# Page visits of up to three units in two banks, joined index sums and key scores, a later hand-over of weight loads and a tail on three engines, in a one-core decoder step

## The chip, the core and the metric

One Trainium2 chip, one of its cores. The metric is the device time of one execution in microseconds (us): the median of several runs, and beside it one execution under the hardware profiler. The engines are TensorE (PE; PEld is its weight load), VectorE (DVE), ScalarE (ACT), GpSimd (POOL) and SyncE (SP), which issues most DMAs.

## The reference

One layer of a decoder step for 256 prompt tokens and 64 sample tokens (8 requests of 8 tokens; NT = 320 columns in all), all in float32. One input projection feeds three groups of heads, and one output projection and a LayerNorm end the layer:

```python
aq, ak, av, ag, iq, ik, iw, bq, bf, bi, bg, mq, mg = _in_proj(h, w_in, pos)      # 2048 -> 8272 columns, rotary on q, k
sc   = _indexer_scores(iq, iw, ik_all)       # sum over 16 heads of w * relu(q . k): the index head sums
_, sel = lax.top_k(sc, n_sel)                # 256 of 2056 keys for a sample token, 64 of 256 for a prompt token
a_out = _sparse_attend(q, k[sel], v[sel], valid)     # 8 heads x 128; a sample token's keys lie in 16 pages of 128
b_o, s = _hgrn2(bq, bf, bi, lb, s0, chunk)   # gated linear recurrence, 4 heads
m_out = _mem_attend(mq, mk, mv)              # cross-attention into 256 memory tokens, 4 heads
cat   = concatenate([a_out * silu(ag), rms(b_o) * silu(bg), m_out * silu(mg)])
y     = layernorm(ALPHA * h + cat @ w_out)
```

The cached keys, values and index keys of the 8 requests are read through a page table; the selection is a mask over all past keys, so every page is read once.

## The kernel before

**Wide work.** The projections run as matmuls of 128x128 weights on 320 (or 256, 512) columns. Each float32 weight is split in two parts (wh and wl, rounded float32r), so each product is three matmuls: wh with xh, wh with xl, wl with xh. A weight entry of 512 KB lands in a buffer `wr` (three of them), ACT casts a half to `wh`, DVE or POOL subtracts to `wl` (four buffers each), and PE uses the halves in quanta of two row blocks. The list `wspec` fixes the order of the entries: input projection with the memory projection in it, then the output projection (`wo`), whose rows come from `cat` after `split` has cut them into the same two parts.

**Narrow work.** The sample tokens of one request pair give 32 columns, so their attention runs as matmuls with 128x32 weights: four groups (two requests, two halves of heads) beside each other. For each of four pairs p there are eight units of keys (K, two pages of each request) and eight of values (V); two units each of cross keys (XK) and cross values (XV) serve the memory. A key unit writes 256 columns of a bank `kv`; two make 512 scores, which ACT copies to S. A value unit adds to the bank `va`. The kernel calls a stretch of units on PE a visit.

**What sets the order.** The kernel writes its program with a planner (`Plan`) that keeps a time for each engine and tile. The main loop at the end asks `units_now` whether a visit of pages is due: before, two units if both are there, one if the next weight half is not ready or it has waited `PATIENCE`. Else PE gets the next quantum of `wspec`. All other work stands in generators in the list `bg`, which `background` resumes when their wants (`need(...)`) are met; a want with `visit=` is held for so many us until a visit comes, and then `join_visit` resumes it right behind the visit. `new_keys` (scores of a pair's 8 new keys against its queries) is such a one; the recurrence and parts of the extraction are others. The index head sums (`sums` in `idx_sample`) are written by the next step of the index scores. `loads` decides what SP issues: a weight goes as soon as `plan.slot_free("wr", 3) <= plan.now + 1`, that is up to 1 us before the planner believes its buffer free; pages go when a buffer `pg` or `S` is free and the planned DMA queue is less than 4 us ahead; at most LOOK units ahead. SP issues in order, so an issue that waits for its buffer holds up what is behind it.

**The tail.** `finish_sample` normalises the last 64 rows, laid out as 128 x 1024 in `r`: DVE subtracts the mean and multiplies by g, and then multiplies by the inverse deviation and adds b, each in a piece of 640 and one of 384 columns, and SP stores each piece.

In the kernel's lines below a helper issues every instruction, so that all stand at one line in the profile (L157 before, L160 after); instructions are told apart by tile names.

Of the kernel before, what the change touches and what calls it, by code (L numbers as in the profile page):

```python
# [36 lines left out]
RES = 7  # L37
PACE = 4.8
HOMES = 5
EARLY = [(2, 1), (2, 3), (2, 5), (2, 6), (2, 7)]  # L40
PATIENCE = 9.0
SOON = 0.4
LAG = 1.5
LAG2 = 0.8
VISIT_WAIT = 9.0
HASTE = 2.0
CALM = 4.0
IDLE = 3.0
LOOK = 3
TABLES = {AF.Exp: "exp_ln", AF.Ln: "exp_ln", AF.Silu: "silu", AF.Sqrt: "sqrt"}  # L50
EXP_LN = 6
PORT = ("tensor_tensor", "tensor_add", "tensor_sub", "tensor_mul", "scalar_tensor_tensor", "tensor_scalar", "tensor_copy",
# [93 lines left out]
class Engine:  # L146
# [41 lines left out]
    def cost(self, op, outs, ins, n):  # L188
        if self.name == "PE":
            n, a = math.prod(outs[0].shape[1:]), ins[0]  # L190
            shape = tuple(next(w for w in (32, 64, 128) if m <= w) for m in (a.shape[0], math.prod(a.shape[1:])))
            turn = 0.0
            if shape != self.shape:
                turn = 0.31 if shape == (128, 128) else 0.09 if self.shape == (128, 128) else 0.2
                self.shape = shape
            if op == "transpose":
                return turn + 0.109
            if a.dtype == F32R:
                return turn + 0.0087 + n * 0.0004325
# [29 lines left out]
def hymba_step(ctx: ExitStack, tc: tile.TileContext, I, O):  # L229
# [483 lines left out]
    def key_scores(p, u, ps):  # L713
# [5 lines left out]
        return  # L719
        yield  # L720

    def unit(n):
        kind, p, u = punits[n]
        tl = [PG.pop((n, b)) for b in range(2)]
# [2 lines left out]
        if kind == "K":  # L727
# [1 line left out]
                S[p] = new([128, PAST + NS], "S")  # L729
                plan.pinned.add(S[p].tensor.name)  # L730
            if u % 2 == 0:
                st["kv"] = PS([128, 512], "kv")
            c = 256 * (u % 2)
            for hh in range(2):
                for h2 in range(2):
# [8 lines left out]
        elif kind == "V":  # L744
            if u == 0:
                VACC[p] = PS([128, 512], "va")
            for j in range(2):
                kt = 2 * u + j
                for b, hp, g in GROUPS:
                    PE.matmul(VACC[p][g:g + 32, :], PTt[p][:, kt, g:g + 32], pair(tl[b][:, j, :], hp),  # L750
                              start=kt == 0, stop=False)
            if u == 7:
                for b, hp, g in GROUPS:
                    PE.matmul(VACC[p][g:g + 32, :], PTt[p][:, 16, g:g + 32], pair(avS, hp),
                              start=False, stop=True)
                bg.insert(0, [extract(p), need(VACC[p], ps=0)])
                done.add(("vdone", p))
        elif kind == "XK":
            if p == 0:
                st["xk"] = PS([128, 512], "kv")  # L760
            ps = st["xk"][:, 256 * p:256 * p + 256]
            for h in range(4):
                for b in range(4):
                    PE.matmul(ps[32 * b:32 * b + 32, :], st["mqpad"][:, 4 * p + b, h, :],
                              tl[b // 2][:, b % 2, 256 * h:256 * h + 256], start=h == 0, stop=h == 3)
            if p == 1:
                for g in range(2):
                    bg.insert(0, [xsoft(g, st["xk"][:, 256 * g:256 * g + 256]), need(st["xk"], ps=0)])
        else:
            va = PS([128, 512], ("va", "kv")[p])  # L770
            for nt in range(2):
                for b in range(4):
                    PE.matmul(va[32 * b:32 * b + 32, :], st["xpt", p][:, nt, 32 * b:32 * b + 32],
                              tl[b // 2][:, b % 2, 512 * nt:512 * nt + 512], start=nt == 0, stop=nt == 1)
            bg.insert(0, [xextract(p, va), need(va, ps=0)])
            if p == 1:
                free(st["mqpad"])

    def unit_ready(n):
# [1 line left out]
        if any((n, b) not in PG or plan.avail(PG[n, b]) > plan.now for b in range(2)):  # L781
            return False
        if kind == "K":
            return u % 2 or ("aq", 7) in done and plan.slot_free("kv", 1) <= plan.now and (
                u or plan.slot_free("S", BUFS["S"]) <= plan.now and len(S) + len(in_s) + ci_live(1) < BUFS["S"]
                and (p < BUFS["S"] or ("soft", p - BUFS["S"]) in done))
        if kind == "V":
# [12 lines left out]
    def units_now(n):  # L800

        if not unit_ready(n):
            return 0
        kind, p, u = punits[n]
        if u % 2 or kind[0] == "X" and p:
            return 1
        if loaded(n + 1) and (kind != "V" or u < 6 or "attn" in done):
            return 2
        if kind[0] == "X":
            return 0  # L810
        if since[0] is None:
            since[0] = plan.now
        return int(not half_soon() or plan.now > since[0] + PATIENCE)

    def half_soon():
        if half >= len(wspec) or half not in WH:
# [100 lines left out]
    def idx_sample():  # L917
# [26 lines left out]
        more = new([128, 2048], "pg")  # L944
        plan.split.add(more.tensor.name)
        st["more"] = 1
        slots = [t[:, 512 * i:512 * i + 512] for t in (early, more) for i in range(4)]
        used = [0]

# [4 lines left out]
        def sums(sp, rs):  # L954

            for c in sorted({c for c, f in rs}):
                ps = PS([128, 512], "va")
                for f in (1, 0):
                    for g in range(4):
                        PE.matmul(ps[32 * g:32 * g + 32, :], wpad[sp][:, g, f, :], rs[c, f][g], start=f == 1, stop=f == 0)  # L960
                d = sc[:, 512 * c:512 * c + 512]
                if sp:
                    DVE.tensor_add(d, d, ps)
                else:
                    ACT.copy(d, ps)

        def new_tokens():

# [48 lines left out]
        while not keys_in(0):  # L1017
            yield
        kk = stack(0)
        rs, full = {}, None  # L1020
        for k, (sp, c, f, a) in enumerate(steps):
            n = kk[0].shape[-1]
            yield need(ql, qh, *kk, ps=2, lag=LAG2)
# [3 lines left out]
                PE.matmul(pd[j][:, 0:n], qh[:, b], kk[j], start=True, stop=False)  # L1027
                PE.matmul(pd[j][:, 0:n], qlr[:, b], kk[j], start=False, stop=True)
            if full:
                sums(*full)  # L1030
                if (sp, c) == (0, 1):
                    new_sums()
                full = None
            r = rs.setdefault((c, f), [])
            for j in range(2):
                r.append(relu_slot(n))
# [2 lines left out]
                else:  # L1039
                    DVE.tensor_scalar(r[-1], pd[j][:, 0:n], 0.0, None, op0=OP.max)  # L1040
            if a == 1 and f == 0:
                full, rs = (sp, rs), {}
            while not keys_in(k + 1):
                yield
            if k + 1 < len(steps):
                kk = stack(k + 1)
                yield
        yield need(*[x for r in full[1].values() for x in r], ps=1)
        sums(*full)
        del st["more"]  # L1050
        free(ql, qh, *st.pop("wpad"))
        done.add("idxdone")
# [148 lines left out]
    def new_keys(p):  # L1201

        yield from wait(("ak", 7))
        while p not in S:
            yield
        yield need(akS, st["qpad"], visit=VISIT_WAIT)
        ps = PS([128, NS])
        for hh in range(2):
            for h2 in range(2):
# [52 lines left out]
    def extract(p):  # L1262
# [2 lines left out]
        o = [T(256), T(256)]  # L1265
        for i in range(2):
            ACT.activation(o[i], VACC[p][:, 256 * i:256 * i + 256], AF.Copy, scale=RS[p][:, 1:2])
        del VACC[p], PTt[p]
        yield from wait(("gate", 7))
        yield need(*o)  # L1270
# [625 lines left out]
    def finish_sample():  # L1896
# [3 lines left out]
        DVE.bn_aggr(out=s[0:64, 0:2], in_=bn[0:64])  # L1900
        ACT.activation(s[0:64, 2:3], s[0:64, 1:2], AF.Sqrt, bias=eps[0:64, 1:2])
        DVE.tensor_copy(s[64:128, 0:1], s[0:64, 0:1])
        for cs in (slice(0, 640), slice(640, 1024)):
            DVE.scalar_tensor_tensor(r[:, cs], r[:, cs], s[:, 0:1], gb[:, 0, cs], op0=OP.subtract, op1=OP.mult)
            if cs.start == 0:
                DVE.reciprocal(s[0:64, 2:3], s[0:64, 2:3])
                ACT.copy(s[64:128, 2:3], s[0:64, 2:3])
        for cs in (slice(0, 640), slice(640, 1024)):
            DVE.scalar_tensor_tensor(r[:, cs], r[:, cs], s[:, 2:3], gb[:, 1, cs], op0=OP.mult, op1=OP.add)
            SP.dma_start(O["ys"][:, cs], r[:, cs])  # L1910


# [122 lines left out]

    asked = {}

    def met(want):
        deps, nps, lag, _ = want
        return all(plan.avail(a) + lag <= plan.now for a in deps) and (not nps or n_free("mA") + n_free("mB") >= nps)  # L2040

    def resume(e):
        asked.pop(e[0], None)
# [7 lines left out]
    def join_visit():  # L2051

        for e in list(bg):
            if e[1] and e[1][3] and met(e[1]):
                resume(e)

    def loads():
        nonlocal nw, npg
        while True:
            if plan.t["SP"] > plan.now + 0.5:  # L2060
                return
            if nw < len(wspec) and wspec[nw].get("ref"):
                nw += 1
                continue
            if nw < len(wspec) and nw < half + 5 and plan.slot_free("wr", 3) <= plan.now + 1 and nw - nprep < 3 \
                    and (wspec[nw]["kind"] != "mem" or has_room(3)):
                load_w(nw)
                nw += 1
# [203 lines left out]
```

## Time and profile before

| | us |
|---|---|
| median of 3 runs | 855.14 (854.65 to 855.36) |
| the profiled execution | 854.57 |
| its span, first to last instruction | 852.8 |
| granted TensorE clock | 0.997 |

Busy time and DMA by stage, from the trace (share of the 16 DMA engines, GB/s):

| stretch, us | PE | DVE | ACT | POOL | DMA | GB/s |
|---|---|---|---|---|---|---|
| 0 to 100 | 98.29 | 78.83 | 52.03 | 54.31 | 0.69 | 225 |
| 100 to 360 | 260.00 | 203.28 | 135.61 | 127.70 | 0.88 | 327 |
| 360 to 480 | 120.00 | 62.23 | 56.96 | 28.56 | 0.99 | 382 |
| 480 to 530 | 50.00 | 29.43 | 25.44 | 14.94 | 1.00 | 382 |
| 530 to 700 | 170.00 | 91.38 | 84.30 | 43.11 | 1.00 | 383 |
| 700 to 730 | 30.00 | 16.47 | 14.84 | 7.87 | 0.78 | 280 |
| 730 to 845 | 114.83 | 67.78 | 52.67 | 47.47 | 0.53 | 165 |

How to read the lines that follow: a row of the timeline is start and duration in us, engine, line, operation, out<-in by tile name, `rows*columns` of the weight, size of what is written, and a count where equal ones are merged. A float32 matmul is recorded twice. Durations of matmuls overlap: what counts on PE is the step from one start to the next.

### The profile page before, as it was taken

How to read it: one execution, taken by the hardware profiler on the slowest of the kernel's cores; microseconds unless marked ns; L12 is line 12 of the kernel's file. 1: busy time of each engine (PE TensorE's matmuls, PEld its weight loads, DVE VectorE, ACT ScalarE, POOL GpSimd, SP SyncE). 2: the span in 40 equal slices, each digit the busy share in tenths (PEclk: the TensorE clock that was granted, in tenths of full speed). 3: DMA queues.
4: the chain of work that ended last, by engine and by line, in shares of the span. 5: the costliest groups of instructions: out<-in, count | busy, mean ns of one | idle time of the engine just before them, and what ended most of it. 6: DMA issues, size and time to landing. Idle time of an engine off the chain costs nothing.

```text
span 852.8 us, 19150 instructions
## 1 busy us (share of the span) xinstructions
PE 843.1 (99%) x6892; PEld 718.0 (84%) x6892; DVE 553.9 (65%) x1100; ACT 422.3 (50%) x908; POOL 326.0 (38%) x333
## 2 busy tenths in 40 slices
PE   9999999999999999999999999999999999999996
PEld 8999999877889898878778788787887889888885
DVE  7788897744897898654474556557545343953655
ACT  6454565553555543634544554554444353744432
POOL 0677562564634445331142214333311110714424
PEclk9999999999999999999999999999999999999998
DMA  9567456889999999999989999999999988756633
GB/s 342 172 189 228 156 172 251 279 307 411 376 389 397 335 327 359 398 360 403 389 330 409 408 353 389 401 397 377 347 409 400 364 324 291 272 171 199 195 99 123
DMA packets 83216, 266.49 MB, mean 312 GB/s; under 512 B 10481, under 2 KB 21170, under 8 KB 82482
## 3 DMA queue, kind: packets, MB, share of 16 engines
q1 hardware_dynamic: 82098, 263.18, 83.6%
q0 software_dynamic: 1024, 2.10, 0.8%
q8 instruction: 54, 0.88, 0.4%
q14 instruction: 40, 0.33, 0.1%
HBM read 256.50 MB, written 8.73 MB: 311 GB/s over the span
## 4 chain that ended last, share of the span: by engine, by line
PE 98%; DMA 1%; DVE 0%; SPq 0%; ACT 0%; DVEq 0%; issue 0%
PE pj L157 57%; PE mB L157 13%; PE va L157 10%; PE mA L157 10%; PE kv L157 8%; DMA S<-in_first 1%; DVE pg L157 0%; SPq L157 0%; ACT xh L157 0%; ACT PT L157 0%; DVE s L157 0%; DVEq L2258 0%; DVE avn L157 0%
## 5 line engine op out<-in xcount | busy, mean ns | idle before, releaser
L157 ACT CAST wh<-wr 128x512 fp32r<-128x512 f32 x334 | 205.0, 621 | 243.5 <-PE pj L157 183.9
L157 PE MATMUL pj<-xh,wh 128*128 128x320 f32 (+1 forms) x992 | 313.6, 316 | 0.0
L157 PE MATMUL pj<-xh,wl 128*128 128x320 f32 (+1 forms) x992 | 303.9, 306 | 0.0
L157 PE MATMUL pj<-xl,wh 128*128 128x320 f32 (+1 forms) x992 | 303.8, 306 | 0.0
L157 DVE TENSOR_TENSOR wl<-wr,wh 128x512 fp32r<-128x512 f32 x222 | 172.7, 785 | 181.9 <-ACT wh L157 166.5
L157 POOL TENSOR_TENSOR wl<-wr,wh 128x512 fp32r<-128x512 f32 x112 | 151.0, 1357 | 240.2 <-ACT wh L157 222.7
L157 PEld LDWEIGHTS pj<-xh,wh 128*128 128x128 f32 x992 | 186.7, 188 | 16.0 <-issue 12.5
L157 PEld LDWEIGHTS pj<-xl,wh 128*128 128x128 f32 x992 | 186.8, 188 | 1.3
L157 PEld LDWEIGHTS pj<-xh,wl 128*128 128x128 f32 x992 | 186.6, 188 | 0.0
L157 POOL TENSOR_TENSOR t<-t,t 128x256 f32<-128x256 f32 (+3 forms) x53 | 46.2, 873 | 119.5 <-ACT t L157 60.0
L157 PE MATMUL va<-pg,PT 128*32 128x512 f32 x456 | 58.4, 595 | 0.0
L157 PE MATMUL kv<-pg,qpad 128*32 128x256 f32 (+1 forms) x916 | 57.5, 380 | 0.0
L157 PEld LDWEIGHTS kv<-pg,qpad 128*32 128x32 f32 (+1 forms) x916 | 30.8, 110 | 20.4 <-issue 1.3
L157 PEld LDWEIGHTS va<-pg,PT 128*32 128x32 f32 x456 | 14.6, 109 | 30.4 <-issue 28.1
L157 DVE MAX8 PT<-PT 128x8 f32<-128x1032 f32 x32 | 39.5, 1234 | 0.5
L157 DVE MATCH_REPLACE8 PT<-PT 128x1032 f32<-128x1032 f32 x32 | 39.0, 1218 | 0.0
L157 POOL DMA_INDIRECT S<-in_ci,row x24 | 25.5, 1064 | 20.0 <-DVE row L157 10.6
L157 PE MATMUL mB<-t,wh 128*128 128x256 f32 x128 | 24.5, 289 | 0.0
L157 POOL TENSOR_TENSOR bp<-t,bp 128x128 f32<-128x128 f32 (+1 forms) x17 | 10.7, 627 | 36.0 <-ACT bp L157 36.0
L157 DVE TENSOR_TENSOR cat<-S,cat 64x512 fp32r<-64x512 f32 x24 | 19.5, 813 | 6.9 <-ACT cat L157 6.4
L157 POOL TENSOR_TENSOR t<-t,tabm 128x320 f32<-128x320 f32 x16 | 14.5, 908 | 24.4 <-DVE t L157 24.2
L157 POOL TENSOR_TENSOR xl<-cat,xh 128x256 fp32r<-128x256 f32 x12 | 12.5, 1061 | 24.8 <-ACT xh L157 24.8
(430 smaller groups left out, 1355.0 us busy)
## 6 DMA issues: line engine op xcount, KB each, us to landing
wr<-in_wt SPq DMA_DIRECT2D x124, 512.0 KB
pg<-in_ck SPq DMA_DIRECT2D x114, 512.0 KB
pg<-in_cv SPq DMA_DIRECT2D x114, 512.0 KB
wr<-in_wo SPq DMA_DIRECT2D x36, 512.0 KB
wr<-in_wm SPq DMA_DIRECT2D x16, 512.0 KB
S<-in_ck SPq DMA_DIRECT2D x14, 512.0 KB
S<-in_cv SPq DMA_DIRECT2D x14, 512.0 KB
pg<-in_cXV SPq DMA_DIRECT2D x8, 512.0 KB
```

Source lines behind the costliest of these rows:

```text
L157: res = f(*a, **k)
```

## The change

- **Visits.** `units_now` lets a visit take up to VISIT = 3 units, and waits for a further one that will land within NEAR = 3 us, unless PATIENCE is over or no weight half is ready. `follows` says which unit may join. LOOK goes from 3 to 4.
- **Two banks.** Once the index scores are done, key units use the banks `kv` and `va` in turn; the accumulator of the values is pinned in `va` meanwhile.
- **Joining.** `sums_at_visit` puts the index head sums into `bg` with a visit's want, and whichever comes first, a visit or the next step, writes them; `new_keys` waits up to 18 us, not 9, for a visit; `join_visit` measures against the end of the visit.
- **Hand-over.** A weight's load is given to SP 0.6 us after the planner believes its buffer free, where it was 1 us before.
- **Planned cost** of a float32r matmul: n/2400 + 0.0133 us, where it was 0.0004325 n + 0.0087.
- **Tail.** DVE centres the last 320 columns first; ACT scales them and POOL adds b, while DVE centres and scales the other 704.

```diff
-LOOK = 3
+TAIL = 320
+VISIT = 3
+NEAR = 3.0
+LOOK = 4
@@ Engine.cost
-                return turn + 0.0087 + n * 0.0004325
+                return turn + 0.0133 + n / 2400
@@
+    def key_bank(u):
+        return ("kv", "va")[u // 2 % 2] if "idxdone" in done else "kv"
@@ unit
-                st["kv"] = PS([128, 512], "kv")
+                st["kv"] = PS([128, 512], key_bank(u))
...
                 VACC[p] = PS([128, 512], "va")
+                plan.pinned.add(VACC[p].tensor.name)
@@ units_now
-        if u % 2 or kind[0] == "X" and p:
-            return 1
-        if loaded(n + 1) and (kind != "V" or u < 6 or "attn" in done):
-            return 2
         if kind[0] == "X":
-            return 0
+            return 1 if p else 2 if loaded(n + 1) else 0
+        k, most = 1, min(VISIT, len(punits) - n)
+        while k < most and loaded(n + k) and follows(n, n + k):
+            k += 1
         if since[0] is None:
             since[0] = plan.now
-        return int(not half_soon() or plan.now > since[0] + PATIENCE)
+        if plan.now > since[0] + PATIENCE or not half_soon():
+            return k
+        if k < most and follows(n, n + k) and all((n + k, b) in PG and plan.avail(PG[n + k, b]) < plan.now + NEAR for b in range(2)):
+            return 0
+        return k if k > 1 else 0
+
+    def follows(n, m):
+        kind, p, u = punits[m]
+        if kind == "V":
+            return u and (u < 7 or "attn" in done)
+        if kind == "K":
+            return u % 2 or u and plan.slot_free(key_bank(u), 1) <= plan.now and (
+                key_bank(u) != key_bank(u - 2) or punits[n][2] == u)
+        return False
@@ idx_sample
+        def sums_at_visit(k, rs):
+            yield need(*[x for r in rs.values() for x in r], visit=VISIT_WAIT)
+            if full and full[0][2] == k:
+                sums(*full.pop()[0:2])
...
             if a == 1 and f == 0:
-                full, rs = (sp, rs), {}
+                full.append((sp, rs, k))
+                if k + 1 < len(steps):
+                    bg.insert(0, [sums_at_visit(k, rs), None])
+                rs = {}
@@ new_keys
-        yield need(akS, st["qpad"], visit=VISIT_WAIT)
+        yield need(akS, st["qpad"], visit=2 * VISIT_WAIT)
@@ finish_sample
-        for cs in (slice(0, 640), slice(640, 1024)):
-            DVE.scalar_tensor_tensor(r[:, cs], r[:, cs], s[:, 0:1], gb[:, 0, cs], op0=OP.subtract, op1=OP.mult)
...
+        centre(rest_c)
+        DVE.reciprocal(s[0:64, 2:3], s[0:64, 2:3])
+        ACT.copy(s[64:128, 2:3], s[0:64, 2:3])
+        ACT.activation(r[:, rest_c], r[:, rest_c], AF.Copy, scale=s[:, 2:3])
+        POOL.tensor_add(r[:, rest_c], r[:, rest_c], gb[:, 1, rest_c])
+        centre(most)
+        DVE.scalar_tensor_tensor(r[:, most], r[:, most], s[:, 2:3], gb[:, 1, most], op0=OP.mult, op1=OP.add)
+        for cs in (most, rest_c):
             SP.dma_start(O["ys"][:, cs], r[:, cs])
@@ join_visit
-            if e[1] and e[1][3] and met(e[1]):
+            if e[1] and e[1][3] and met(e[1], max(plan.now, plan.t["PE"] - 0.4)):
@@ loads
-            if nw < len(wspec) and nw < half + 5 and plan.slot_free("wr", 3) <= plan.now + 1 and nw - nprep < 3 \
+            if nw < len(wspec) and nw < half + 5 and plan.slot_free("wr", 3) <= plan.now + (-0.6) and nw - nprep < 3 \
```

What this does to the order of the instructions, at three places.

PE, in the key pages, the new key scores of two pairs (akS is the tile of new keys, qpad that of the padded queries, 32x64 what one writes; pj is the input projection). Before, between two products of the projection:

```order
L157 MATMUL pj_3362<-xl,wh_3356 128x320
L157 MATMUL pj_3362<-xh,wl_3357 128x320
L157 MATMUL mB_3474<-akS,qpad_411 32x64 x16
L157 MATMUL mA_3491<-akS,qpad_411 32x64 x16
L157 MATMUL pj_3362<-xh,wh_3356 128x320
```

After, right behind a visit of two key units, the first in bank kv and the second in va; the end of the second and what follows:

```order
L160 MATMUL va_3432<-pg_3174,qpad_411 32x256 x2
L160 MATMUL va_3432<-pg_3239,qpad_411 32x256 x2
L160 MATMUL mB_3449<-akS,qpad_411 32x64 x16
L160 MATMUL mA_3466<-akS,qpad_411 32x64 x16
L160 MATMUL pj_3345<-xh,wh_3317 128x320
L160 MATMUL pj_3345<-xl,wh_3317 128x320
```

The two groups moved from a stretch of their own to the end of a stretch of pages. The same holds for the other two pairs.

PE, at the change from the input projection (pj) to the output projection (mA<-wh,xh). Before, the last rows of the one and the first of the other; the transposes that extract the last cross values (ident) stand 132 products ahead of these, and the visit of the cross values 144:

```order
L157 MATMUL pj_9673<-xh,wh_9669 128x320
L157 MATMUL pj_9673<-xl,wh_9669 128x320
L157 MATMUL pj_9673<-xh,wl_9670 128x320
L157 MATMUL mA_9777<-wh_9690,xh 128x512
L157 MATMUL mA_9777<-wh_9690,xl 128x512
L157 MATMUL mA_9777<-wl_9691,xh 128x512
```

After, the transposes stand right between the two:

```order
L160 MATMUL pj_9621<-xl,wh_9611 128x320
L160 MATMUL pj_9621<-xh,wl_9612 128x320
L160 MATMUL mA_9770<-ident,t_9730 128x128 x2
L160 MATMUL mA_9770<-ident,t_9731 128x128 x2
L160 MATMUL mA_9797<-wh_9640,xh 128x512
```

and the visit itself (va from tiles S and pg, 32x512) stands between the last weight but one (wh_9572 is its last half) and the last (wh_9592 and wh_9611):

```order
L160 MATMUL pj_9621<-xh,wh_9572 128x320
L160 MATMUL pj_9621<-xl,wh_9572 128x320
L160 MATMUL pj_9621<-xh,wl_9573 128x320
L160 MATMUL va_9672<-S_9415,t_9543 32x512 x2
L160 MATMUL va_9672<-pg_9455,t_9543 32x512 x2
```

So the visit moved from 144 wide products ahead of the output projection to 24 ahead of it.

SP, in the key pages (wr is a weight's buffer, pg a page's, in_ck the cached keys, ISA the setting of a page's address). Before:

```order
L157 DMA wr_2122<-in_wt 128x1024
L157 TENSOR_LOAD ptab x3
L157 DMA wr_2169<-in_wt 128x1024
L157 DMA out_kT<-t_2125 128x320
L157 ISA
L157 DMA pg_2190<-in_ck 128x1024
```

After:

```order
L160 DMA wr_2112<-in_wt 128x1024
L160 TENSOR_LOAD ptab x3
L160 ISA
L160 DMA pg_2159<-in_ck 128x1024
L160 ISA
L160 DMA pg_2159<-in_ck 128x1024
L160 DMA wr_2174<-in_wt 128x1024
```

The page moved ahead of the second weight.

More of the change, by code (lines that the diff above doesn't have):

```diff
@@ L783, in unit_ready @@
         if kind == "K":
-            return u % 2 or ("aq", 7) in done and plan.slot_free("kv", 1) <= plan.now and (
+            return u % 2 or ("aq", 7) in done and plan.slot_free(key_bank(u), 1) <= plan.now and (
                 u or plan.slot_free("S", BUFS["S"]) <= plan.now and len(S) + len(in_s) + ci_live(1) < BUFS["S"]
@@ L946, in idx_sample @@
         st["more"] = 1
+        full = []
         slots = [t[:, 512 * i:512 * i + 512] for t in (early, more) for i in range(4)]
@@ L965, in sums @@
                     ACT.copy(d, ps)
+            if (sp, c) == (0, 1):
+                new_sums()
+        def sums_at_visit(k, rs):
+            yield need(*[x for r in rs.values() for x in r], visit=VISIT_WAIT)
+            if full and full[0][2] == k:
+                sums(*full.pop()[0:2])
         def new_tokens():
@@ L1019, in idx_sample @@
         kk = stack(0)
-        rs, full = {}, None
+        rs = {}
         for k, (sp, c, f, a) in enumerate(steps):
@@ L1029, in idx_sample @@
             if full:
[L1030 to L1033, printed above, removed]
+                sums(*full.pop()[0:2])
             r = rs.setdefault((c, f), [])
@@ L1041, in idx_sample @@
             if a == 1 and f == 0:
-                full, rs = (sp, rs), {}
+                full.append((sp, rs, k))
+                if k + 1 < len(steps):
+                    bg.insert(0, [sums_at_visit(k, rs), None])
+                rs = {}
             while not keys_in(k + 1):
@@ L1047, in idx_sample @@
                 yield
-        yield need(*[x for r in full[1].values() for x in r], ps=1)
-        sums(*full)
+        yield need(*[x for r in full[0][1].values() for x in r], ps=1)
+        sums(*full.pop()[0:2])
         del st["more"]
@@ L1267, in extract @@
             ACT.activation(o[i], VACC[p][:, 256 * i:256 * i + 256], AF.Copy, scale=RS[p][:, 1:2])
+        plan.pinned.discard(VACC[p].tensor.name)
         del VACC[p], PTt[p]
@@ L1902, in finish_sample, with centre @@
         DVE.tensor_copy(s[64:128, 0:1], s[0:64, 0:1])
-        for cs in (slice(0, 640), slice(640, 1024)):
+        tail = 1024 - TAIL
+        most, rest_c = slice(0, tail), slice(tail, 1024)
+        def centre(cs):
             DVE.scalar_tensor_tensor(r[:, cs], r[:, cs], s[:, 0:1], gb[:, 0, cs], op0=OP.subtract, op1=OP.mult)
[L1905 to L1909, printed above, removed]
+        centre(rest_c)
[6 more added lines that the diff above has]
+        for cs in (most, rest_c):
             SP.dma_start(O["ys"][:, cs], r[:, cs])
@@ L2036, in hymba_step, with met @@
     asked = {}
-    def met(want):
+    def met(want, now=None):
         deps, nps, lag, _ = want
-        return all(plan.avail(a) + lag <= plan.now for a in deps) and (not nps or n_free("mA") + n_free("mB") >= nps)
+        return all(plan.avail(a) + lag <= (now or plan.now) for a in deps) and (not nps or n_free("mA") + n_free("mB") >= nps)
     def resume(e):
```

## Prediction

> **What bounds the kernel now.** I read the head of the page first, then its chain of work that ended last.
>
> ```profile
> span 852.8 us, 19150 instructions
> PE 843.1 (99%) x6892; PEld 718.0 (84%) x6892; DVE 553.9 (65%) x1100; ACT 422.3 (50%) x908; POOL 326.0 (38%) x333
> ...
> PE 98%; DMA 1%; DVE 0%; SPq 0%; ACT 0%; DVEq 0%; issue 0%
> ```
>
> TensorE is busy from start to end and the chain never leaves it for long. A busy PE is no proof by itself, since matmul ends are modelled, so I asked for PE's own waits. There are two, both within the first 11 us:
>
> ```profile
> PE kv L1947 <- DVE t L157: 1.1, 1, 1.1
> PE va L157 <- ACT PT L157: 0.6, 1, 0.6
> ```
>
> So the time is the sum of the steps from one matmul's start to the next one's, plus about 8 us of tail. No matmul is removed by the change. Its effect can come from three things only: fewer changes between wide matmuls (128*128) and narrow ones (128*32), waits of PE that go or come, and the tail.
>
> **The price of a visit.** A visit is a run of narrow matmuls between wide ones. This is the timeline of PE around one that computes index head sums, start first:
>
> ```profile
> 203.22 0.31 PE L157 MATMUL pj<-xh,wh 128*128 128x320 f32 x1
> ...
> 204.39 0.31 PE L157 MATMUL pj<-xh,wl 128*128 128x320 f32 x1
> 204.63 0.63 PE L157 MATMUL va<-cat,t 128*32 128x512 f32 x3
> ...
> 205.09 0.60 PE L157 MATMUL va<-cat,t 128*32 128x512 f32 x3
> ...
> 205.94 0.60 PE L157 MATMUL va<-pg,t 128*32 128x512 f32 x3
> ...
> 206.49 0.41 PE L157 MATMUL pj<-xh,wh 128*128 128x320 f32 x1
> 206.74 0.31 PE L157 MATMUL pj<-xl,wh 128*128 128x320 f32 x1
> ```
>
> A wide step is (204.39 - 203.22)/8 = 0.146 us. Narrow matmuls start four at a time (three from cat and one from pg in these rows), and each of them is recorded twice, so the visit of eight is four sets; from 205.09 to 205.94 are two, 0.425 each. From 204.39 to 206.74 are 2.35 us; two wide steps (0.29) and four sets (1.70 to 1.72) leave **0.34 us** that the change of shape costs, on the way in, on the way out and in the first wide step after it.
>
> **Visits, counted.** In PE's order before I count 46 visits: 17 of key pages (cross keys among them), 18 of value pages, 4 of index head sums, 3 of new key scores, 4 of the recurrence. After: 18, 17, 4, 0 and 3, so 42. Two things stand out. Only two visits take three units (both of values), and the key visits, now spread over two banks, have become one more. And the index head sums still stand in four visits of their own: where they come due, no page visit stands between them and the next step of the scores, which adds them itself. What joined are the new key scores of all pairs, and one group of the recurrence. **4 x 0.34 = -1.36 us.**
>
> Against it stands that a visit that ends in transposes is cheaper to leave. Here PE comes straight from a key visit:
>
> ```profile
> 254.54 0.55 PE L157 MATMUL mA<-ident,t 128*128 128x128 f32 x3
> 254.84 0.39 PE L157 MATMUL pj<-xh,wh 128*128 128x320 f32 x1
> 255.07 0.31 PE L157 MATMUL pj<-xl,wh 128*128 128x320 f32 x1
> ```
>
> The first wide step takes 0.23 (254.84 to 255.07) where it took 0.25 above (206.49 to 206.74). I take 0.05 in all for such an exit, since the rows don't show what of the way out the transposes hide as well (an estimate; its bounds are 0.02, and 0.17, half the price). Nine visits end so, in transposes or mask matmuls, before, and seven after: **+0.1** (0.04 to 0.34).
>
> **Waits on the path.** In the stretch where the output projection begins there is a small one that the list of PE's waits, which leaves out gaps under its limit, shows at the weight load only:
>
> ```profile
> PEld mA L157 <- POOL wl L157: 0.5, 1, 0.5
> ```
>
> and that PE's timeline has there as two long steps:
>
> ```profile
> 736.26 0.39 PE L157 MATMUL mA<-wh,xl 128*128 128x512 f32 x1
> 736.68 0.50 PE L157 MATMUL mA<-wl,xh 128*128 128x512 f32 x1
> 737.01 0.39 PE L157 MATMUL mB<-wh,xh 128*128 128x512 f32 x1
> ```
>
> 0.42 and 0.33, where such a step takes 0.23 (0.146 x 512/320): 0.3 us. Here ACT, DVE and POOL split cat for the projection and prepare weights together. After, the cross value visit stands between the last two weights of the input projection, so the split, which starts when the first of these is through, has that visit (about 4 us) more ahead of the projection. Against it, ACT loads a table more there. I take **-0.2** (0 to -0.3).
>
> **Hand-over of weights.** The load of a weight buffer is now given to SP 1.6 us later by the planner's clock. Before, it is given so early that SP stands waiting for the buffer:
>
> ```profile
> SPq L157 <- DVE wl L157: 154.2, 79, 6.3
> SPq L157 <- POOL wl L157: 129.3, 54, 6.5
> ```
>
> 133 waits of 2.1 us on average (the columns are us in total, times, the longest), with every page, store and number of a page queued behind. 1.6 us of later hand-over comes out of them for the most part, so a weight lands little later, and what stands behind it sooner. And there is stock:
>
> ```profile
> ACT wh L157 <- PE pj L157: 183.9, 166, 4.9
> ACT wh L157 <- DMA wr<-in_wt: 11.2, 8, 2.1
> ```
>
> ACT's casts wait 166 times for PE to give a buffer back, 8 times for a weight: a load that is up to 1.6 us late is covered by that stock. **0 us**. If the cover were gone, a late weight would cost PE up to 1.6 us; on the other side stand at most the 0.8 us that PE's weight loads wait for value pages (row in the second rival), which an earlier page could take away. Later bank changes, the pins on the accumulator and the longer visit wait of the new keys issue nothing on PE that is not counted.
>
> **The shared tail.** Before, DVE alone centres and scales 640 and 384 columns:
>
> ```profile
> L157 DVE SCALAR_TENSOR_TENSOR pg<-pg,s,pg 128x640 f32<-128x640 f32 x2 | 1.8, 878 | 0.0
> L157 DVE SCALAR_TENSOR_TENSOR pg<-pg,s,pg 128x384 f32<-128x384 f32 x2 | 1.2, 599 | 0.0
> ```
>
> The timeline has their order, and SP's the issue of the two stores:
>
> ```profile
> 846.84 0.89 DVE L157 SCALAR_TENSOR_TENSOR pg<-pg,s,pg 128x640 f32<-128x640 f32 x1
> 847.64 0.15 DVE L157 RECIPROCAL s<-s 64x1 f32<-64x1 f32 x1
> 847.72 1.92 DVE L157 SCALAR_TENSOR_TENSOR pg<-pg,s,pg 128x384 f32<-128x384 f32 x3
> ```
>
> ```profile
> 849.13 0.86 SPq L157 DMA_DIRECT2D out_ys<-pg  x2
> ```
>
> A column costs (878 - 599)/256 = 1.09 ns, so 320 take 0.53 us and 704 take 0.95; each starts 0.07 to 0.09 before the last ends. After: centre 320 from 846.84, reciprocal 847.29, centre 704 from 847.37, scale 704 from 848.24 to 849.19. The larger store is issued at 849.22, against 849.13. So the share given away buys nothing on the path: before, the first store waited for 640 + 384 + 640 columns, now for 320 + 704 + 704, 64 more. ACT's copy and scale of 320 columns end about 848.25 (reciprocal done 847.44, copy 0.2, scale 0.5 to 0.6), and then POOL's add comes up against DVE:
>
> ```profile
> 842.57 1.30 POOL L157 TENSOR_TENSOR S<-S,pg 128x512 f32<-128x512 f32 x1 [4.49 <-ACT S L157]
> ...
> 843.82 1.95 POOL L157 TENSOR_TENSOR S<-S,pg 128x512 f32<-128x512 f32 x1
> ```
>
> and on DVE at the time of the second:
>
> ```profile
> 843.97 0.67 DVE L157 TENSOR_TENSOR S<-S,pg 128x512 f32<-128x512 f32 x1
> ```
>
> The same POOL add took 1.30 alone and 1.95 with a DVE add of 0.67 in it: one stood for the other. If DVE's scale (848.24) is first, POOL's add (1.30 x 320/512, 0.8 to 0.9) ends near 850.1 and the smaller store goes at 850.1, against 849.66, into a queue in which the larger still moves: **+0.1** on the end, +0.45 at most if the end follows the second issue.
>
> [...]
>
> **Sum.** -1.36 + 0.1 - 0.2 + 0 + 0.1 = -1.4 us. The profiled execution took 854.57, 0.6 under the median of the three runs (855.14), with 1.8 us outside its span; it would take 853.2, and the median becomes **853.7 us**. A measurement of this kernel can tell about 0.2%, 1.7 us, from no change, so this lies just inside "no change".
>
> **Rivals.**
> 1. It gains more: the wait at 736 goes whole, exits and tail cost nothing: -1.36 - 0.3 = -1.7, 853.4, on the border of what can be told. The runs before spread over 0.7 us, so a true -1.4 can also be measured beyond it. For it: PE is the whole chain, so every saved switch counts. Against: no row has a fifth visit to save.
> 2. Slower, through late pages. In the stretch of the value visits the DMA engines are full, and three visits already begin on the landing of a tile:
>
> ```profile
> 530.00:700.00 170.00, 170.00 (x1489) 135.36 (x1482) 91.38 (x202) 84.30 (x206) 43.11 (x50) 1.00 1.00 383
> ```
>
> (the last two figures of a stretch are the DMA engines' share and GB/s), and
>
> ```profile
> PEld va L157 <- DMA pg<-in_cv: 0.8, 3, 0.3
> ```
>
> After, the last visits stand nearer to the output projection: 24 wide matmuls lie behind the cross values, 144 before. PE's order is fixed, so if the stream of pages slips by one unit (two tiles of 1.05 MB, 5.5 us at 383 GB/s), PE stands for it: -1.4 + 5.5, 859.2. It decides from 3.1 us of waits on. Against: SP is freer, and the planner orders the visits by the landing of pages.
> [...]
> 4. The change does not do what it says. For the sums this is so by PE's order, and counted above; had the four joined too, it would be another -1.36, 852.3.
>
> **How the numbers follow.** The forecast (853.0 to 854.3) has 0.43, the first rival 0.30 (half of it the spread of runs), the third 0.15, the second 0.12. The range reaches from 852.6, the first rival with the 0.8 us of page waits gone, to 856.5, the third rival with one weight late (1.6) and the dearer exits (0.3); what the second gives above that lies outside. Faster by over 0.2%: 0.30; within: 0.58; slower: 0.12.
>
> **What would show it.** Right: PE's wide steps 0.146 as now, the new key scores without a wide matmul ahead of them, 0.34 us less for each joined group; no wait of PE near the first projection matmuls; DVE's two 704-column steps end near 4.3 us after the last matmul ends, POOL's add behind them. Wrong: PE waits for pg, S or wr tiles, a wait of over 1 us anywhere after 11 us, or a tail over 0.5 us longer. If the time falls by more than 2 us, the price of a visit or the count of what PE waits for was too small.

## The result, and the profile after

| | before | after |
|---|---|---|
| median of 6 runs each, us | 854.89 (854.36 to 855.52) | 861.52 (860.50 to 862.41) |
| the profiled execution, us | 854.57 | 860.91 |
| its span, us | 852.8 | 859.2 |

The ratio is 1.0076, 95% interval 1.0066 to 1.0086: slower by 6.6 us, where 853.7 was forecast. The head of the page and its chain of work that ended last:

```profile
span 859.2 us, 19158 instructions
PE 845.2 (98%) x6892; PEld 721.2 (84%) x6892; DVE 550.8 (64%) x1095; ACT 426.3 (50%) x911; POOL 330.0 (38%) x338
...
PE 36%; DVE 1%; ACT 0%; issue 0%; ACTq 0%; DVEq 0%
```

PE does the same 6892 matmuls in 2 us more of busy time, and a span 6.4 us longer. The chain is followed back only some 320 us here (its shares add up to 37%), but it now runs through DVE and ACT, which means that PE waited for them. The list of PE's waits says so outright (us in total, times, the longest):

```profile
PE mB L160 <- ACT t L160: 1.9, 1, 1.9
PE kv L1983 <- DVE t L160: 1.1, 1, 1.1
PE va L160 <- ACT PT L160: 0.8, 1, 0.8
PE mB L160 <- DVE s L160: 0.5, 1, 0.5
PE mA L160 <- DVE s L160: 0.4, 1, 0.4
```

The second and third stand in the first 11 us, as before. The first is new. None is for a page or for a weight to land; two more rows of 0.2 us follow in the list, one of them for ACT's cast of a weight. PE's timeline at the new wait:

```profile
591.76 0.71 PE L160 MATMUL mA<-bp,t 128*128 128x512 f32 x2
594.42 0.73 PE L160 MATMUL mB<-bp,t 128*128 128x512 f32 x2 [1.95 <-ACT t L160]
594.99 0.42 PE L160 MATMUL pj<-xh,wh 128*128 128x320 f32 x1
595.21 0.47 PE L160 MATMUL pj<-xl,wh 128*128 128x320 f32 x1
595.48 0.47 PE L160 MATMUL pj<-xh,wl 128*128 128x320 f32 x1
595.74 0.47 PE L160 MATMUL pj<-xh,wh 128*128 128x320 f32 x1
...
598.41 0.33 PE L160 MATMUL pj<-xh,wh 128*128 128x320 f32 x1
598.58 0.31 PE L160 MATMUL pj<-xl,wh 128*128 128x320 f32 x1
```

Two things are to be seen. The two state updates of the recurrence (mA<-bp,t and mB<-bp,t, twice 512 columns each) stand right behind each other, and the second waits 1.95 us. And the wide steps behind it take 0.26 to 0.27 (595.21 to 595.48 to 595.74) where such a step takes 0.15. The table by stretches (length, busy time of PE, PEld, DVE, ACT and POOL, then the granted clock, the DMA share and GB/s) tells why:

```profile
592.00:594.00 2.00, 0.47 (x2) 0.03 (x1) 1.49 (x6) 0.76 (x3) 0.62 (x1) 1.00 1.03 399
594.00:596.00 2.00, 1.58 (x6) 1.49 (x7) 1.10 (x5) 0.70 (x2) 0.00 (x0) 0.76 1.02 376
596.00:598.00 2.00, 2.00 (x7) 1.61 (x7) 0.32 (x2) 0.15 (x1) 0.00 (x0) 0.50 1.01 374
598.00:600.00 2.00, 2.00 (x14) 2.00 (x13) 0.55 (x1) 1.47 (x3) 0.46 (x1) 0.89 1.02 297
```

PE's clock is granted at half for 3.4 us after the wait (0.24, 0.50 and 0.11 of three stretches of 2 us of PE's clock are lost, which is 1.7 us). What kept ACT and DVE:

```profile
592.51 1.12 DVE L160 SCALAR_TENSOR_TENSOR bp<-bp,eG,mA 128x128 f32<-128x128 f32 x4 [1.42 <-PE mA L160]
593.55 0.75 DVE L160 COPY t<-mB 128x256 f32<-128x256 f32 x2
```
```profile
593.99 0.70 ACT L160 COPY t<-mB 128x256 f32<-128x256 f32 x2 [1.25 <-DVE t L160]
```

The two banks mB still hold the memory keys. Their copies stand on DVE behind the four updates of the first half, which wait for PE's first state update. So PE asks for a bank that can't be empty before its own last work has gone through DVE.

The tail after (DVE, ACT, POOL, SP, one timeline, cut):

```profile
850.07 0.28 PE L160 MATMUL kv<-wl,qpad 128*128 128x256 f32 x1
...
852.33 0.55 DVE L160 SCALAR_TENSOR_TENSOR pg<-pg,s,pg 128x320 f32<-128x320 f32 x1
...
852.87 2.57 DVE L160 SCALAR_TENSOR_TENSOR pg<-pg,s,pg 128x704 f32<-128x704 f32 x2
...
853.84 0.86 POOL L160 TENSOR_TENSOR pg<-pg,pg 128x320 f32<-128x320 f32 x1 [1.37 <-DVE pg L160]
855.47 0.81 SPq L160 DMA_DIRECT2D out_ys<-pg  x2
```

Both 704-column steps should end 1.9 after 852.87; they end 2.57 after it. Taken apart, the first took 0.92, and the second, recorded from 853.89 on, 1.55. From the last matmul's start to the end of the span are 859.2 - 850.1 = 9.1 us, before 852.8 - 844.6 = 8.2.

### The profile page after: what moved, and what is told of

It is laid out like the page before. It is cut to its first block, busy times and chain, and to the rows that moved or that the text cites. A ratio compares the mean times of both kernels' runs of the same rounds, so it can differ in the third digit from the quotient of the medians.

```text
span 859.2 us, 19158 instructions
## 1 busy us (share of the span) xinstructions
PE 845.2 (98%) x6892; PEld 721.2 (84%) x6892; DVE 550.8 (64%) x1095; ACT 426.3 (50%) x911; POOL 330.0 (38%) x338
## 5 line engine op out<-in xcount | busy, mean ns | idle before, releaser
L160 DVE TENSOR_TENSOR wl<-wr,wh 128x512 fp32r<-128x512 f32 x222 | 170.8, 779 | 181.4 <-ACT wh L160 173.5
L160 POOL TENSOR_TENSOR t<-t,t 128x256 f32<-128x256 f32 (+3 forms) x58 | 51.3, 885 | 119.0 <-DVE t L160 61.0
L160 PE MATMUL kv<-pg,qpad 128*32 128x256 f32 x580 | 34.1, 380 | 0.0
L160 PEld LDWEIGHTS kv<-pg,qpad 128*32 128x32 f32 x580 | 19.6, 110 | 12.0 <-issue 2.4
L160 POOL TENSOR_TENSOR bp<-t,bp 128x128 f32<-128x128 f32 (+1 forms) x19 | 12.8, 673 | 30.4 <-ACT bp L160 30.3
L160 PE MATMUL va<-pg,qpad 128*32 128x256 f32 x368 | 24.2, 380 | 0.0
L160 DVE TENSOR_TENSOR cat<-S,cat 64x512 fp32r<-64x512 f32 x24 | 17.2, 715 | 10.6 <-ACT cat L160 10.1
```

Source lines behind the costliest of these rows:

```text
L160: res = f(*a, **k)
```

## The experiments

Each was timed in several rounds beside the kernel before on its chip; the ratio is to that. "Both repairs" are those of the first two runs together.

| run | what it is | median us | ratio to before, 95% interval |
|---|---|---|---|
| e1 | after, bank repair | 858.17 | 1.0037 (1.0023 to 1.0050) |
| e2 | after, old tail | 860.10 | 1.0064 (1.0050 to 1.0077) |
| e3 | after, old price of a wide matmul | 868.40 | 1.0151 (1.0137 to 1.0165) |
| e4 | before, new tail | 855.61 | 1.0007 (0.9998 to 1.0016) |
| e5 | after, both repairs | 857.54 | 1.0031 (1.0019 to 1.0044) |
| e6 | e5, one key bank | 857.49 | 1.0028 (1.0018 to 1.0038) |
| e7 | e5, early hand-over | 865.99 | 1.0116 (1.0095 to 1.0137) |
| e8 | before, bank repair and joins | 864.52 | 1.0108 (1.0092 to 1.0123) |
| e9 | before, bank repair and later hand-over | 858.09 | 1.0037 (1.0023 to 1.0050) |
| e10 | before, bank repair, joins, new price, later hand-over | 863.74 | 1.0099 (1.0084 to 1.0114) |
| e11 | e6 with the old price | 863.82 | 1.0103 (1.0088 to 1.0119) |
| e12 | e5 without three table loads | 856.66 | 1.0019 (1.0010 to 1.0028) |

**e1, the planner's book of banks.** `Plan.slot` gives a new tile the bank whose last use is oldest, and enters the old tile's time as the new one's. When the two accumulators of the memory keys are claimed at once, the first carries the older of two old times, and the second strikes the first from the list. This is the planner's own record of it (its clock):

```
mB_1076 now 529.614 takes mB_1021 last 505.539   other in use: mB_1022 505.95
mB_1077 now 529.614 takes mB_1076 last 505.539   other in use: mB_1022 505.95
mB_1245 now 591.632 takes mB_1022 last 505.947   other in use: mB_1077 593.91
```

So at 591.6 it believed mB_1022's bank free, while the chip's bank still held mB_1076. The kernel before strikes a tile off in the same way (mB_1083 at 535.2 by the planner's clock), but claims the next bank mB only at 607.4, when the other of that pair had been read, at 603.3.

```diff
-                pj["m"] = [PS([128, 512], w) for w in ("mB", "mB", "pj", "pj")]
+                pj["m"] = []
+                for w in ("mB", "mB", "pj", "pj"):
+                    pj["m"].append(PS([128, 512], w))
+                    plan.r[pj["m"][-1].tensor.name] = plan.now
```

> The changed kernel with one correction in the planner's book of PSUM banks: the two accumulators of the memory keys are entered as in use from the moment they are claimed, so that the second doesn't strike the first off the list. The order is the changed kernel's up to the second state update of the recurrence at 592 us, which then finds its bank really taken and stands later. Theory A (the planner believed a bank free that was still to be read; PE stood 1.95 us for it, and its clock then ran at half for nearly 4 us): the wait and the slow stretch go, 2.1 + 1.7 = 3.8 us less than the changed kernel, about 857.7 us, mean granted clock back at 0.997. Rival B (the bank is not the cause; DVE and ACT are late there anyway, and PE will wait for them at the next place): 0 to 1 us less, 860.5 to 861.5, and a wait of over 1 us on DVE or ACT between 585 and 605 us. Rival C (the wait goes, but the slow clock had another cause): 2.1 us less, 859.4.

Measured 858.17, 3.35 less than the changed kernel. PE now puts six wide matmuls between the two updates and takes a bank mA:

```profile
593.93 0.71 PE L160 MATMUL mA<-bp,t 128*128 128x512 f32 x2
594.48 0.31 PE L160 MATMUL pj<-xh,wh 128*128 128x320 f32 x1
...
595.36 0.62 PE L160 MATMUL mA<-bp,t 128*128 128x512 f32 x2
```

The wait and the half clock are gone (granted clock of the run 0.997). Theory A holds, 0.4 short of its size. The profiled execution, at 859.24 the longest of the five, has another wait that the changed kernel's doesn't have, 0.9 us for ACT at 488 us, ahead of the repaired place.

**e2 and e4, the tail.** The old tail in the changed kernel, and the new tail in the kernel before:

```diff
-        centre(rest_c)
-        DVE.reciprocal(...); ACT.copy(...)
-        ACT.activation(r[:, rest_c], r[:, rest_c], AF.Copy, scale=s[:, 2:3])
-        POOL.tensor_add(r[:, rest_c], r[:, rest_c], gb[:, 1, rest_c])
-        centre(most)
-        DVE.scalar_tensor_tensor(r[:, most], ...)
+        for cs in (slice(0, 640), slice(640, 1024)):   # both steps on DVE
...
```

> The changed kernel with the tail of before (DVE alone centres and scales 640 and 384 columns). All else is as in the changed kernel. [...] Rival B (the tail differs by the larger share of DVE alone, 64 columns, 0.1 us): 861.4.

> The kernel before with the new tail alone. [...] Rival B (only the 64 columns more on DVE count): 855.0, ratio 1.000.

e2: 860.10, 1.4 less; e4: 855.61 beside 854.76 in the same group, 0.85 more, though its interval reaches no change. The traces leave no doubt on the size: from the last matmul's start to the end are 8.2 us with the old tail (before and e2) and 9.1 with the new (after), 0.9 apart, where rival B had 0.1; the span of e4 is 853.9, of before 852.8. e2 keeps the wait at the state update, with a difference:

```profile
592.85 0.71 PE L160 MATMUL mA<-bp,t 128*128 128x512 f32 x2
595.51 0.73 PE L160 MATMUL mB<-bp,t 128*128 128x512 f32 x2 [1.95 <-ACT t L160]
596.08 0.31 PE L160 MATMUL pj<-xh,wh 128*128 128x320 f32 x1
596.22 0.31 PE L160 MATMUL pj<-xl,wh 128*128 128x320 f32 x1
...
597.94 0.31 PE L160 MATMUL pj<-xh,wh 128*128 128x320 f32 x1
```

The same wait, and no slow step behind it. From the second update to the same wide matmul are 597.94 - 595.51 = 2.43 us here and 598.41 - 594.42 = 3.99 above: where the half clock follows, it costs 1.6 us more. That half clock was missing in this execution of e2 can be why it gained more than the tail's 0.9.

**e3, the price of a wide matmul.** One number of the planner back to its old value:

```diff
-                return turn + 0.0133 + n / 2400
+                return turn + 0.0087 + n * 0.0004325
```

> The changed kernel with the planner's old price of a wide matmul (0.0087 us and 0.4325 ns a column in place of 0.0133 us and 1/2400 us a column: 1.5% dearer at 512 columns). Theory A (the old price was a hidden margin: the planner's clock fell 5 us behind the chip in the course of the kernel, so what it believed ready was ready; the new price takes the margin away): the waits of PE after 11 us go back from 7.5 to about 3 us, with the half clock gone, and the time falls by 4 to 5 us less 3 visits more (44 against 41, 1.0 us): 857 to 858.5. Rival B (the waits come from the new order of the visits, whatever the price): the waits stay between 5 and 9 us, time 860 to 864.

Measured 868.40: both times missed, and theory A has fallen. A new wait leads the list:

```profile
PE va L160 <- DMA S<-in_ck: 3.5, 1, 3.5
```

The old price is no margin. The waits of PE after 11 us add up to 7.7 us, as rival B said, and the clock ran at half for 10.2 us, which rival B didn't count. The old price makes the planner believe PE later than it is: in its record the last matmuls of the kernel before stand some 5 us too late, measured from the first. That PE therefore comes to the page before it has landed is argued and not shown. By 508 us, ahead of the late page, the old price had moved the planner's clock, measured against the traces, only 1.1 us from where it stood in the changed kernel, and e10 below has late pages with the new price.

**e5, both repairs.**

> The changed kernel with both repairs: the two accumulators of the memory keys entered as in use when claimed, and the tail of before. Theory A (bank and tail are separate and add up): 861.5 - 3.4 - 0.85 = 857.3 us, still 2.4 above the kernel before; left over are the other waits (about 2 us more than before, most of it between 500 and 560 and between 715 and 740 us) and visits that save 0.6 in place of 1.26. Rival B (the waits shift from place to place, the repairs don't add up): 858.2 or more. Rival C (the two were all that was wrong, the rest is spread): 853.7.

857.54, which is 4.0 us less than the changed kernel, where theory A said 4.2; taken singly the two repairs gave 3.35 and 1.4. Single executions lie between 856.06 and 858.93, and the interval reaches to 858.7, so rival B's 858.2 isn't excluded.

**e6, one key bank** (`key_bank` returns "kv" always).

> As the run with both repairs, but all key scores in one bank as before (key_bank gives kv always). PE's order has 41 visits as with two banks, and five stretches fewer that leave the wide matmuls (93 against 98; transposes stand beside visits again). Theory A (a group of transposes that stands alone costs 0.1 to 0.3 us more than beside a visit): 0.5 to 1.5 us less than with two banks, 856 to 856.8. Rival B (the second bank spares waits for the eviction of the first): slower than with two banks, 857.5 or more, with waits of PE for DVE or ACT at the key visits (150 to 360 and 500 to 545 us).

857.49, no difference, and no wait of PE for the eviction of a key bank: neither theory. The second bank neither costs nor brings anything that shows.

**e7 to e11, other parts alone.** Their edits are those of the diff, taken back or made alone (e7: `plan.now + 1`; e8: `sums_at_visit`, `2 * VISIT_WAIT` and the shift in `join_visit` alone; e9: `plan.now + (-0.6)` alone; e10: those of e8 and e9 with the new price; e11: the old price). e8 to e10 have the old rule for visits, LOOK = 3 and one key bank; all five have the old tail and the bank repair.

> As the run with both repairs, but with the early hand-over of weight loads of before (plan.now + 1). PE's order has 43 visits against 41. Theory A (the hand-over itself costs nothing, only the two visits count, 0.7 us, and the order of the rest is a matter of luck): 857 to 859. Theory B (the later hand-over makes weights late and so the waits on ACT and DVE): waits of PE after 11 us back to about 2 us as before, 856 or less.

> The kernel before (its tail, hand-over, price of a wide matmul, visits of two units, one key bank) with the bank repair and the joins alone: index head sums and new key scores wait longer for a visit, and what is to join may come due until 0.4 us before PE ends the visit. PE's order has 43 visits against 45 and one stretch more. Theory A (a joined visit is worth 0.34 us, as the rows of before say, and no wait comes): 854.9 - 0.7 + 0.1 = 854.3, ratio 0.9993. Rival B (any new order brings waits of PE of 1 to 5 us, since DVE and ACT stand close behind PE in places): 856 or more.

> The kernel before (its tail, price, visits, joins) with the bank repair and the later hand-over of weight loads alone. PE's order has 45 visits, as before, and 98 stretches that leave the wide matmuls against 94. Theory A (the later hand-over costs and brings nothing by itself, as predicted; four stretches more of transposes cost 0.1 to 0.3 each): 855.3 to 856. Theory B (the new orders need it because it lets pages past the waiting weight loads, but before has no late page that it could help): the same time, and no wait of PE for DMA; SP's waits for DVE and POOL to give a weight buffer back fall from 283 us to well under 250. Rival C (any new order brings waits of 1 to 5 us on DVE and ACT): 857 or more, with those waits in the list.

> Of the change only the joins, the exact price of a wide matmul and the later hand-over, with the bank repair and the tail of before; visits of at most two units by the old rule and one key bank. PE's order has 43 visits and 95 stretches. Theory A (with exact price and later hand-over together no page is late; what remains is two visits saved, 0.7 us, less what waits on ACT and DVE the order brings, 0 to 3 us): no wait of PE for DMA, 854.3 to 857. Rival B (the rule for three units with its look ahead is what keeps pages in time): a wait of PE of 1 to 4 us for a page, 858 or more.

> Of the change the joins, the new rule for visits and the later hand-over, with the bank repair, the tail of before, one key bank, and the old price of a wide matmul. PE's order has 44 visits and 92 stretches. Theory A (the old price is dearer than the chip, so that the planner's clock falls behind by up to 8 us and visits are set before their pages are there on the chip): PE waits 2 to 4 us for a page between 500 and 700 us, 858 to 864. Rival B (the old price did harm only together with two banks): no wait for DMA, 854 to 857.

All five are slower than the kernel before, by 3 to 11 us, and in all five PE waits for a key page inside a visit. e7's list and e9's timeline:

```profile
PE kv L160 <- DMA pg<-in_ck: 2.8, 1, 2.8
...
PE va L160 <- DMA pg<-in_ck: 1.4, 1, 1.4
```
```profile
228.11 2.35 PE L160 MATMUL kv<-pg,qpad 128*32 128x256 f32 x36
233.67 1.71 PE L160 MATMUL kv<-pg,qpad 128*32 128x256 f32 x26 [3.21 <-DMA pg<-in_ck]
```

e8 has 2.6 us of it, e10 4.3 in three waits, e11 3.3 (for S). Both theories of e7 are wrong (857 to 859, and 856 or less). Rival B of e8 holds in part: waits for DVE of 1.0 and 1.3 us came, as it said, but the longest is for a page. Rival B of e10 and theory A of e11 hold in time and in the wait, though not shown in their reasons. All of e9 are wrong: in the profiled execution, which took 858.95, the late page is 3.2 of some 4 us, and DVE and ACT, which rival C named, are not in the list after 11 us. SP's waits for weight buffers, which the later hand-over was to cut, did not fall: 151.1 us for DVE and 137.6 for POOL in e9, 289 together, and 283.5 before. Only the combinations that hold the new visit rule, the new price and the later hand-over together (after, e1, e2, e5, e6, e12), and the kernel before with either tail, have no wait for pages over 0.3 us. Why a page is late in the others is open; each of these edits changes the planner's whole order.

**e12, ACT's table loads.** After, ACT loads a table ten times, before eight; the last load stands in front of the output projection:

```profile
735.29 1.28 ACT L160 ACT_TABLE_LOAD   x1
736.58 1.55 ACT L160 ACTIVATE t<-t 128x320 f32<-128x320 f32 x4
738.04 2.17 ACT L160 CAST wh<-wr 128x512 fp32r<-128x512 f32 x4
```

and PE there:

```profile
738.10 0.39 PE L160 MATMUL mB<-wl,xh 128*128 128x512 f32 x1
738.70 0.50 PE L160 MATMUL mA<-wh,xh 128*128 128x512 f32 x1 [0.21 <-ACT wh L160]
739.04 0.40 PE L160 MATMUL mA<-wh,xl 128*128 128x512 f32 x1
739.42 0.50 PE L160 MATMUL mA<-wl,xh 128*128 128x512 f32 x1
```

```diff
-            res = f(*a, **k)
+            res = f(*(a[:2] + (AF.Exp,) + a[3:] if plan.last_gate and op == "activation" and a[2] == AF.Silu else a), **k)
```

> As the run with both repairs, in the same order on every engine, but three of ACT's ten table loads are gone, the last two of them at 711.8 and 731.6 us: the gates from the fifth chunk on are passed through the exponential, whose table is loaded anyway, in place of the Silu (these gates are computed otherwise, the rest is as it was). Theory A (the order that sets the cross softmax between two groups of gates makes ACT load tables twice more, and PE waits for what ACT then does late): the wait for the softmax at 716.5 us (0.7) and the long steps at 734 to 736 us (0.75) go, 1.3 us less than with them: 856.2 us and a span of about 853.3. Rival B (ACT's casts there wait for PE to give weight buffers back, whatever is loaded): within 0.3 us of the run with both repairs, and the waits stay.

This kernel leaves the Silu of these gates out, so it doesn't compute the layer; it is there for the order and the times. PE at the same place (the steps at 738.70 and 739.04 above):

```profile
736.49 0.39 PE L161 MATMUL mA<-wh,xh 128*128 128x512 f32 x1
736.72 0.39 PE L161 MATMUL mA<-wh,xl 128*128 128x512 f32 x1
```

The load before the gates is gone, and with it the long steps (0.23 each in the whole stretch, 0.75 us less); the gates themselves take 1.55 us as above. The load before the cross softmax stayed, since it is written out in the program, and so did that wait. The median, 856.66, is 0.9 below that of e5, but the intervals of the two ratios overlap, so the trace shows the gain and the medians alone do not. Half of theory A is shown, its other half wasn't tried.

## Why the prediction was wrong

**What failed.** The prediction said that the time is the sum of PE's steps and that the change acts through fewer switches, "waits of PE that go or come", and the tail; but waits that come were counted at one place, 736 us, and at weights and pages. The sentence that later bank changes and longer visit waits "issue nothing on PE that is not counted" is the step that failed: PE's order was read for its visits, and not for which bank the next matmul takes and who must empty it. In place of that nothing the runs show a wait of 2.1 us for DVE and ACT to empty a bank, with 1.6 us of half clock behind it (e1). No rival named DVE or ACT as what PE would wait for, and no term held a slower clock.

| term, us | predicted | trace of after |
|---|---|---|
| four visits fewer, dearer exits | -1.26 | -1.2 |
| start of the output projection | -0.2 | +0.45 |
| hand-over of weights | 0 | no wait in the trace; taken back alone (e7), it goes with 4.2 us of late pages |
| tail | +0.1 | +0.9 |
| wait at the second state update | - | +2.1 |
| half clock behind it | - | +1.6 |
| wait for the cross softmax, at 720 (mB <- DVE s) | - | +0.5 |
| what is left of 6.4, in steps of 0.1 to 0.5, not taken apart | - | +2.1 |

**The price of a visit was right.** These rows of before show a key visit and the new key scores apart (from the last wide matmul ahead to the second behind):

```profile
501.49 0.31 PE L157 MATMUL pj<-xh,wl 128*128 128x320 f32 x1
501.73 0.65 PE L157 MATMUL mA<-akS,qpad 128*32 128x64 f32 x32
...
502.57 0.31 PE L157 MATMUL pj<-xl,wh 128*128 128x320 f32 x1
...
515.14 0.31 PE L157 MATMUL pj<-xh,wl 128*128 128x320 f32 x1
515.38 1.93 PE L157 MATMUL kv<-pg,qpad 128*32 128x256 f32 x32
...
519.22 0.31 PE L157 MATMUL pj<-xl,wh 128*128 128x320 f32 x1
```

and these of after show them joined:

```profile
521.75 0.31 PE L160 MATMUL pj<-xh,wl 128*128 128x320 f32 x1
521.99 3.66 PE L160 MATMUL kv<-pg,qpad 128*32 128x256 f32 x64
525.47 0.63 PE L160 MATMUL mA<-akS,qpad 128*32 128x64 f32 x32
...
526.28 0.31 PE L160 MATMUL pj<-xl,wh 128*128 128x320 f32 x1
```

Less two wide steps (0.29) each, apart 0.79 + 3.79, joined 4.24: 0.34 saved. A fit of all stretches that leave the wide matmuls in seven profiles (0.01 us of scatter) gives 0.17 for the way in and 0.17 for the way out, 0.15 where transposes follow, and so -1.2 for the whole change: four ways in fewer, and of the ways out seven fewer into transposes and three more straight into wide matmuls. The gain is there, and it is small beside one wait.

**The start of the output projection** was a gain in the sum and is a loss (0.75 of long steps, shown at e12, where before had 0.3): the split does start earlier, but the cross softmax now stands between two groups of gates, and the table load that was named and not priced (1.28 us) puts the casts of the weights behind it. e12 shows this.

**The tail** cost 0.9, where the sum has 0.1. What came is POOL's add ahead of DVE's last scale, which the chances call the third (0.15) and for which the upper end of the range, 856.5, has 0.9: the add started at 853.84, within 0.1 of the time at which DVE would have begun its second step, and took 0.86; that step took 1.55, where the first took 0.92. This is 0.6 of the 0.9; the 64 columns more on DVE and the gap of 0.1 before its second step are most of the rest. The sum gave the order to DVE on a margin of 0.1 us that no row could bear. That POOL's add held DVE up is read from these times: no run moved it alone.

**The late pages** are the second rival. They did not come in the changed kernel, but in six of the twelve runs (e3, e7 to e11) they are the largest wait, 2.6 to 4.3 us. "The planner orders the visits by the landing of pages", said against them, did not keep them away there. "1.6 us of later hand-over comes out of these waits" was wrong too: SP's waits did not fall (296 us after).

**What stays open.** e12, the nearest of those in the changed order, is still 1.6 us over the kernel before. Its trace has what is left in steps of 0.1 to 0.6 us between 320 and 720 us, some in one execution and not in the next. No run took them apart. No version beat the kernel before.

## What to carry to other kernels

Where one engine is busy all the time, a change of order is priced by what each of its instructions then finds, not by how many there are: for every pair that moves closer together, look up which buffer the second takes and what must empty it. A planner's book is part of the kernel: one wrong entry in it stayed without effect until an order came in which it was used. And parts of a change of order need not work singly: the second bank and the new tail could be taken back without harm, but e3 and e7 to e11, which leave out the new visit rule, the new price or the later hand-over, are all slower than the kernel before, and five of the six slower than the whole change.

## What the runs showed of the hardware

**The granted clock.** In the traces of after and of the experiments PE stood eleven times for 1.9 to 3.5 us without a matmul. With seven of these waits the clock was granted at half for 3.4 or 6.8 us, with four not at all, and the length didn't decide it: 1.95 us brought it in the changed kernel and not in e2, and the 3.21 of e9 did not bring it. Single waits of up to 1.3 us never did, but two of 0.86 and 1.35 us, close behind each other, did (e7, from 208.7 to 211.5 us).

Where the wait lay may count as well; no run shows it alone. In the changed kernel's trace the granted clock changes at 595.04, 598.45 and 854.45 us: 3.41 us apart, and 256.00, which is 75 times 3.413. Read from the granted clock of stretches of 2 us, the half clock begins in e3 at 532.4 and 600.6 us and in e7 at 212.2 and 652.5 us, 20 and 129 such times apart. Counted from these changes in stretches of 3.413 us (an estimate), the whole 1.95 us of the changed kernel lay in one, and so did some 2.0 of the 2.79 us of e7 at 526 us, which brought no half clock. So these figures give no limit, and why the 1.95 us of e2 brought none is not shown.

**Twice the price.** At the state update the wait of 2.1 us on the bounding engine cost 3.7, with the 1.6 us of half clock behind it; the same wait in e2 had no half clock behind it.
